# Twelve of sixteen output tiles of a mixer's output projection by the seven-product scheme, with the weight sums added in DRAM

## The chip, the cores and the metric

The kernel runs on one core of one Trainium2 chip. The metric is device time in microseconds (us), the median of several runs. The core has five engines that matter here: TensorE (PE; PEld is its weight load), VectorE (DVE), ScalarE (ACT), GpSimd (POOL) and SyncE (SP, which here only issues DMAs). All arithmetic is in fp32.

## The reference, cut to what matters

One decoder layer on 512 tokens of width 2048: a mixer of three head groups, a cross-attention into 256 memory tokens, and a gated MLP.

```python
def hybrid_mixer(h, w_in, ..., w_out):
    ...
    mixed = jnp.concatenate([o_a, o_b, o_c], axis=-1)     # 512 x 2048
    return mixed @ w_out                                   # w_out 2048 x 2048

mem_n = rms_norm(mem, mem_norm)                            # 256 x 2048
x = x + hybrid_mixer(rms_norm(x, norm_mix), ...)
x = x + memory_cross_attention(rms_norm(x, norm_cross), mem_n, w_cq, w_ckv, w_co)
x = x + conv_ffn(rms_norm(x, norm_ffn), w_up, conv_w, conv_b, w_down)
return rms_norm(x, norm_final)
```

## The kernel before, in words

Activations lie transposed, features on the 128 partitions and tokens along the row, as tiles of 128 x 512. A matmul loads a 128 x 128 block of weights and streams 512 tokens past it. For fp32 accuracy each operand is split in two parts of lower precision (fp32r): a rounded part `hi`, made by ScalarE as a copy, and the rest `lo`, made by VectorE as a subtraction. Each product is then three matmuls (`mm3`, L375 to L377): hi x hi, hi x lo, lo x hi. So each half of a weight tile that comes in (128 x 512, half of a 512 KB DMA) costs one ScalarE and one VectorE operation (`weights` L361 and L362, `split_weights` L336 and L337).

The stages, in order: the input projections; from about 310 us the attention of groups A and B, spread by `tick` between the matmuls of their projections; from 604 us the output projection (`mixer`, its end); the cross-attention (`cross`); the MLP's up projection and its down projection (`ffn`).

**The output projection.** Its 16 output tiles of 128 features each sum over 16 feature tiles of `mixed`. The first half of tiles 0 to 3 runs beside the last attention work; then the attention's memory is closed and the second half of tiles 0 to 3 follows, then tiles 4 to 15 one after the other (`out_units`, two units of 8 blocks each). Each tile is evicted by `evac_o`, which calls `resid` (L1073: VectorE adds the residual x, read from DRAM into a tile `xraw`) and `square` (the sum of squares for the next norm; ScalarE squares, VectorE adds the odd tiles and GpSimd the even ones, L1096). The operands `xo` are the split tiles of `mixed`; they sit in the ring `xp` (`xslot`, tiles `xhi` and `xlo`) that all stages before used for the split x as well.

**The memory's rounding** (`memory`) splits the 16 tiles of the cross-attention's memory (L328, L329), squares them and makes their norm. It is a generator that is advanced one step after each unit from tile 8 on. Its results are needed by the first key tile of the cross-attention (`w_ck`), right after the output projection.

**Queues and buffers.** SP issues the weight loads into a ring of five raw tiles (`WR = 5`, tag `wraw`); the x tiles of the residual use the same ring. Split halves have five buffers each (`WS = 5`). The order on each engine is fixed when the program is built: it follows the order of the program, and an operation that comes later can move up where an engine would be idle and its inputs are there. `issue_after` and `behind` add an order.

**The seven-product scheme.** The MLP's up projection is already computed by it (`up`, `product`): two output tiles, two input tiles and two token halves make a 2 x 2 block product, done with 7 products of 256 tokens in place of 8. It needs sums of weight tiles and sums of token halves. For a few output tiles the weight sums are made ahead in DRAM by DMAs that accumulate, issued by GpSimd, each waiting for the one before (`added`, `up_sums`, L1316); two such sets run at the start of group A's attention (`up_sums(2)` and `up_sums(3)`), one, `up_sums(1)`, behind the sums for the first output tile (`first_sums`, L1362 and L1366), which start with the last square of the output projection. During the cross-attention's output GpSimd also issues accumulating DMAs for squares (L1254).

**Places in memory.** Pools stack from both ends of a partition's memory. A few tiles that nobody reads (`edge`, `ledge`, `rim`, `sill`, `step`) shift what lies behind them by multiples of 32 or 64 bytes.

Of the kernel before, what the change touches and what calls it, by code (L numbers as in the profile page):

```python
# [12 lines left out]
F32 = mybir.dt.float32  # L13
F32R = mybir.dt.float32r
# [5 lines left out]
P = 128  # L20
# [33 lines left out]
EARLY = 4  # L54
BELOW = 3 * PHASE
# [120 lines left out]
def _pack(inp):  # L176
# [26 lines left out]
    a["w_o"] = _units_out(w_out, r(D))  # L203
# [30 lines left out]
class _Trunk:  # L234
    def __init__(self, tc, es, d, out):
# [8 lines left out]
        edge.tile([P, 8], F32, name="edge")  # L244
# [190 lines left out]
    def stats(self, parts, n, name, pool=None):  # L435
# [8 lines left out]
        rs = self.con.tile([P, tl], F32, name="rs" + name)  # L444
        nc.vector.tensor_scalar(rs, ss[:, :tl], 1.0 / D, EPS, op0=ALU.mult, op1=ALU.add)
        nc.gpsimd.tensor_tensor(rs, rs, self.mhalf[:, :tl], op=ALU.pow)

        def spread():
            bc = self.pst("T")
            for t in range(tl):  # L450
                dg = (pool or self.pre).tile([P, P], F32, name="diag", tag="diag", bufs=tl)
                nc.vector.tensor_scalar(dg, self.ident, rs[:, t:t + 1], None, op0=ALU.mult)
                nc.tensor.matmul(bc[:, t * P:(t + 1) * P], self.ones, dg, start=True, stop=True)
            big = (pool or self.con).tile([P, n], F32, name="R", tag="R", bufs=1)
            nc.scalar.activation(big, bc[:, :n], AF.Copy)
            return big

        return rs, spread
# [422 lines left out]
    def mixer(self):  # L881
# [6 lines left out]
        self.vvp = self.pool(es_vv, "vvp", "right")  # L888
        gl = self.pool(es_gl, "gl", "right")
# [90 lines left out]
        for f in range(2, EARLY):  # L980
            self.up_sums(f)
# [17 lines left out]

        def evac_o(dt):  # L1000
            def f(ps):
                self.resid(dt, ps, None, sqs, lambda n: self.mp.tile([P, n], F32, name="sqt", tag="sqt", bufs=2))
            return f
# [9 lines left out]
        units = [self.out_units(d["w_o"], n, xo, evac_o(n), box=box) for n in range(KT)]  # L1013
        self.rate = W_O / 2
        for n in range(0, 4, 2):
# [15 lines left out]
        self.flush()  # L1031
        es_ab.close()
        es_vv.close()
        self.kv = self.pool(self.es_kv, "kv", "right")
        self.kv.tile([P, PHASE], F32, name="ledge")
        self.mp = self.pool(self.es_mp, "mp", "right")
        for n in range(4):
            units[n][1]()
        mem = self.memory()
        for n in range(4, KT):  # L1040
            for u in units[n]:
                u()
                if n >= M0:
                    next(mem, None)
        for _ in mem:
            pass

    def memory(self):

        nc, mp = self.nc, self.mp  # L1050
        parts = [mp.tile([P, MEM], F32, name="msq%d" % i) for i in range(2)]
        self.mem = []
        for k in range(KT):
            if k % 4 == 0:
                four = mp.tile([P, 4, MEM], F32, name="mraw", tag="mraw", bufs=1)
                nc.sync.dma_start(out=four, in_=self.d["memT"][k // 4])
            raw = four[:, k % 4, :]
            hi = mp.tile([P, MEM], F32R, name="mhi%d" % k)
            lo = mp.tile([P, MEM], F32R, name="mlo%d" % k)
            self.mem.append(self.split_to(hi, lo, raw, self.gain(4, k)))  # L1060
            self.square(k, raw, parts, lambda n: mp.tile([P, n], F32, name="msqt", tag="msqt", bufs=2))
            if k % 4 == 3:
                yield
        self.mrs, spread = self.stats(parts, MEM, "m", mp)
        yield
        self.mR = spread()
        yield
# [34 lines left out]
    def cross(self):  # L1102
        nc, d, tc = self.nc, self.d, self.tc
        es = ExitStack()
        kv, mp = self.kv, self.mp
        kh, kl = {}, {}

        def evac_k(h):
            def f(ps):
                kf = mp.tile([P, MEM], F32, name="kf", tag="kf", bufs=2)  # L1110
                nc.vector.tensor_tensor(kf, ps[:, :MEM], self.mR, op=ALU.mult)
                kh[h] = kv.tile([P, MEM], F32R, name="ckh%d" % h)
                kl[h] = kv.tile([P, MEM], F32R, name="ckl%d" % h)
# [4 lines left out]
        vh = [kv.tile([P, S], F32R, name="cvh%d" % i) for i in range(MT)]  # L1118
        vl = [kv.tile([P, S], F32R, name="cvl%d" % i) for i in range(MT)]
# [125 lines left out]
        sx.tile([P, PHASE], F32, name="rim")  # L1245
# [45 lines left out]
        s1, s5 = [self.con.tile([P, HT], F32, name=n) for n in ("s1", "s5")]  # L1291
# [42 lines left out]

    def down_sums(self):
# [18 lines left out]
    def first_sums(self):  # L1354
# [13 lines left out]
        self.up_sums(1)  # L1368
# [496 lines left out]
```

## Time and profile before

| | us |
|---|---|
| median of 3 runs | 2252.03 |
| lowest, highest | 2250.52, 2253.88 |
| profiled execution | 2251.13 |
| its span, first to last instruction | 2249.3 |

| engine | busy, us | share of the span |
|---|---|---|
| TensorE, matmuls | 2232.6 | 99% |
| TensorE, weight loads (beside them) | 2089.9 | 93% |
| VectorE | 1819.5 | 81% |
| ScalarE | 1231.7 | 55% |
| GpSimd | 221.3 | 10% |

The granted clock of TensorE was 0.998 over the span. Busy time of matmuls is a union of overlapping records: the records of a matmul of 256 columns last 277 ns on the mean, though the next one starts after some 114. So the cost of a matmul is read from the distance of starts, or from a count in a window in which TensorE was never idle, not from the mean duration. In rows of groups the two numbers behind the bar are the group's busy time in us and the mean duration in ns; behind the second bar stands the idle time in front of it and what ended it. In rows in order of time the two numbers in front are the start and the duration in us.

### The profile page before, as it was taken

Reading aid. Unit: us, or ns where it says so; the run is one execution under the profiler, and the core shown is the slowest. Engines: PE = TensorE matmul, PEld = TensorE weight load, DVE = VectorE, ACT = ScalarE, POOL = GpSimd, SP = SyncE. Lnnn points to the kernel's source line nnn. Section 1 sums busy time; section 2 is a strip of 40 time slices with the busy share of each in tenths; the row PEclk is TensorE's granted clock in tenths of the full one; section 3 lists DMA queues with packets and bytes.
Section 4 is the critical chain, followed back from the end, with each engine's and each line's share of the span. In section 5 each row is a group of like instructions: output and inputs, shape, how many; then the busy total and the mean of one; then the engine's idle time right before and its main releaser. Section 6 shows DMA issues by size and latency. Waiting matters only on the chain.

```text
span 2249.3 us, 42619 instructions
## 1 busy us (share of the span) xinstructions
PE 2232.6 (99%) x15898; PEld 2089.9 (93%) x15898; DVE 1819.5 (81%) x3587; ACT 1231.7 (55%) x2532; POOL 221.3 (10%) x308
## 2 busy tenths in 40 slices
PE   9999999999999999999999999999999999999997
PEld 8898898888888888889999999999999999999997
DVE  7826756666787356699999999999999999989887
ACT  7324445555575245585555555555555575747563
POOL 2000101000002011121111111111000020101003
PEclk9999999999999999999999999999999999999999
DMA  6422157222224359589777777877534493837542
GB/s 223 162 96 82 49 150 193 97 89 99 78 92 140 122 161 241 134 206 282 198 212 201 221 208 213 215 219 224 173 132 144 145 344 104 305 124 233 186 129 82
DMA packets 141842, 377.09 MB, mean 168 GB/s; under 512 B 14484, under 2 KB 53732, under 8 KB 140932
## 3 DMA queue, kind: packets, MB, share of 16 engines
q1 hardware_dynamic: 90144, 274.18, 35.1%
q0 software_dynamic: 45728, 89.86, 18.2%
q10 hardware_dynamic: 5764, 10.35, 1.3%
q8 instruction: 124, 2.03, 0.4%
q14 instruction: 82, 0.67, 0.1%
HBM read 347.28 MB, written 91.80 MB: 195 GB/s over the span
## 4 chain that ended last, share of the span: by engine, by line
PE 96%; DVE 2%; ACT 1%; DMA 0%; issue 0%; POOL 0%; SPq 0%; DVEq 0%; ACTq 0%
PE acc L375 19%; PE acc L377 19%; PE acc L376 19%; PE psC L375 5%; PE psC L376 5%; PE psC L377 5%; PE acc L416 3%; PE acc L418 3%; PE acc L417 3%; PE psD L377 3%; PE psD L376 3%; PE psD L375 3%; PE psT L556 1%; PE psQ L377 1%; PE psQ L375 1%; PE psQ L376 1%
## 5 line engine op out<-in xcount | busy, mean ns | idle before, releaser
L336 ACT ACTIVATE whi<-wraw 128x512 fp32r<-128x512 f32 (+1 forms) x822 | 471.1, 603 | 407.3 <-PE acc L376 145.0
L337 DVE TENSOR_TENSOR wlo<-wraw,whi 128x512 fp32r<-128x512 f32 (+1 forms) x822 | 522.3, 656 | 65.9 <-ACT whi L336 61.2
L375 PE MATMUL acc<-sum,whi 128*128 128x256 f32 x1956 | 541.8, 277 | 0.4 <-ACT s L1465 0.3
L377 PE MATMUL acc<-sum,wlo 128*128 128x256 f32 x1956 | 541.5, 277 | 0.0
L376 PE MATMUL acc<-sum,whi 128*128 128x256 f32 x1956 | 541.4, 277 | 0.0
L362 DVE TENSOR_TENSOR wlo<-wraw,whi 128x512 fp32r<-128x512 f32 (+2 forms) x328 | 216.1, 665 | 191.2 <-ACT whi L361 188.8
L375 PEld LDWEIGHTS acc<-sum,whi 128*128 128x128 f32 x1956 | 367.2, 188 | 1.0 <-ACT s L1465 0.8
L377 PEld LDWEIGHTS acc<-sum,wlo 128*128 128x128 f32 x1956 | 367.3, 188 | 0.4 <-DVE wlo L337 0.2
L376 PEld LDWEIGHTS acc<-sum,whi 128*128 128x128 f32 x1956 | 367.3, 188 | 0.1
L361 ACT ACTIVATE whi<-wraw 128x512 fp32r<-128x512 f32 (+2 forms) x328 | 198.5, 610 | 284.3 <-PE acc L376 186.5
L375 PE MATMUL acc<-xhi,whi 128*128 128x512 f32 (+1 forms) x848 | 335.1, 395 | 0.5 <-ACT fg L926 0.5
L377 PE MATMUL acc<-xhi,wlo 128*128 128x512 f32 (+1 forms) x848 | 328.4, 387 | 0.0
L376 PE MATMUL acc<-xlo,whi 128*128 128x512 f32 (+1 forms) x848 | 327.9, 387 | 0.0
L375 PE MATMUL psC<-sum,whi 128*128 128x256 f32 x928 | 256.9, 277 | 0.0
L376 PE MATMUL psC<-sum,whi 128*128 128x256 f32 x928 | 256.8, 277 | 0.0
L377 PE MATMUL psC<-sum,wlo 128*128 128x256 f32 x928 | 256.5, 276 | 0.0
L377 PEld LDWEIGHTS acc<-xhi,wlo 128*128 128x128 f32 x848 | 159.3, 188 | 32.5
L375 PEld LDWEIGHTS acc<-xhi,whi 128*128 128x128 f32 x848 | 159.4, 188 | 29.9 <-ACT fg L926 0.9
L376 PEld LDWEIGHTS acc<-xlo,whi 128*128 128x128 f32 x848 | 159.7, 188 | 29.0 <-DVE xlo L324 0.2
L377 PEld LDWEIGHTS psC<-sum,wlo 128*128 128x128 f32 x928 | 174.3, 188 | 0.0
L375 PEld LDWEIGHTS psC<-sum,whi 128*128 128x128 f32 x928 | 174.3, 188 | 0.0
L376 PEld LDWEIGHTS psC<-sum,whi 128*128 128x128 f32 x928 | 174.2, 188 | 0.0
(401 smaller groups left out, 4319.0 us busy)
## 6 DMA issues: line engine op xcount, KB each, us to landing
wraw<-in_w_up SPq DMA_DIRECT2D x125, 512.0 KB, 6.3
b<-in_w_up SPq DMA_DIRECT2D x42, 512.0 KB, 4.5
wraw<-in_w_o SPq DMA_DIRECT2D x32, 512.0 KB, 3.5
wraw<-in_w_d SPq DMA_DIRECT2D x32, 448.0 KB, 4.3
wraw<-in_w_d SPq DMA_DIRECT2D x36, 384.0 KB, 5.0
wraw<-in_w_qka SPq DMA_DIRECT2D x24, 512.0 KB, 3.5
up<-in_w_up POOLq DMA_DIRECT2D x24, 512.0 KB, 7.0
one<-in_w_d POOLq DMA_DIRECT2D x24, 448.0 KB, 6.7
```

Source lines behind the costliest of these rows:

```text
L336: nc.scalar.activation(hi, r, AF.Copy)
L337: nc.vector.tensor_tensor(lo, r, hi.bitcast(F32), op=ALU.subtract)
L361: nc.scalar.activation(hi, r, AF.Copy)
L362: nc.vector.tensor_tensor(lo, r, hi.bitcast(F32), op=ALU.subtract)
L375: nc.tensor.matmul(out, lh, rh, start=start, stop=False, skip_group_check=more)
L376: nc.tensor.matmul(out, lh, rl, start=False, stop=False, skip_group_check=more)
L377: last = nc.tensor.matmul(out, ll, rh, start=False, stop=stop, skip_group_check=more)
L416: self.nc.tensor.matmul(o, xh[:, tt], wh, start=(k == 0), stop=False)
L417: self.nc.tensor.matmul(o, xh[:, tt], wl, start=False, stop=False)
L418: self.last = self.nc.tensor.matmul(o, xl[:, tt], wh, start=False, stop=(k == KT - 1))
L556: nc.tensor.transpose(tp[:, b * P:(b + 1) * P], pt[:, b * P:(b + 1) * P], self.ident)
```

## The change

Tiles 0 to 3 (`PLAIN`) stay as they were. Tiles 4 to 15 become three groups of four (`quad`), each two pairs of output tiles. A pair needs 7 products of 8 blocks x 3 matmuls, with 256 tokens each. The two pairs of a group take turns: product 1 of the first pair, product 1 of the second, and so on.

- The weights' four plain parts come from a new layout `w_p`; the four sums are made in DRAM by `out_sums`, in four sets (two row groups x two column halves) of eight DMAs, at the place where `up_sums(2)` and `up_sums(3)` were. `up_sums(2)` follows them; `up_sums(3)` moves behind `up_sums(1)` in `first_sums`.
- The token sums for products 5, 6 and 3 go to new tiles (`ring`, `low`), and that of product 7 over one half of the `xo` tiles (`place`). `token_turns` makes them in 16 steps: four behind the third plain tile's matmuls, the others while the first group runs, a step after each product. ScalarE copies two or three partial results per pair out of PSUM, VectorE combines the others, and `out` loads x (one tile per output tile, from the raw ring) and adds the residual.
- The groups run their products in the order 1, 2, 4, 5, 6, 3, 7; the last group in the order 5, 6, 3, 7, 1, 2, 4. `memory` now runs in this last group, from its fourth product on in program order, in those tiles; what is left of it runs right behind the group.
- `edge` grows from 8 to 24 floats, and all tiles of `xp` move by 64 bytes; `ledge` in front of `kv` and `rim` go, and a `ledge` of 48 floats is added in the pool `vvp`.

```diff
+PLAIN = 4
+QUADS = (KT - PLAIN) // 4
+LOW = ((5, 3, 0), (5, 3, 1), (3, 3, 0), (3, 3, 1))
+LAST_ORDER = (5, 6, 3, 7, 1, 2, 4)
+OUT_ORDER = (1, 2, 4, 5, 6, 3, 7)
...
-        edge.tile([P, 8], F32, name="edge")
+        edge.tile([P, 8 + PHASE], F32, name="edge")
...
-        for f in range(2, EARLY):
-            self.up_sums(f)
+        self.out_sums()
+        self.up_sums(2)
...
+        for n in range(PLAIN):
+            w = self.weights(d["w_o"][2 * n + 1])
...
+            if n == PLAIN - 2:
+                turns = self.token_turns([self.mix[m] for m in order], xo)
+                for _ in range(4):
+                    next(turns)
+        for n in range(PLAIN):
+            evac_o(n)(box[n])
+        for c in range(QUADS):
+            last = c == QUADS - 1
+            self.quad(PLAIN + 4 * c, LAST_ORDER if last else OUT_ORDER, self.memory() if last else turns)
...
+    def token_turns(self, raw, xo):
...
+        def part(j, v):
+            k = 4 * v
+            if j == 5:
+                a[v] = temp()
+                pair(a[v], lambda i: (raw[k + 2 * i + 1][:, hi], raw[k + 2 * i][:, hi]), ALU.subtract)
...
+            split(j, v)
...
+        def place(v):
+            for i in range(2):
+                th, tl = [t[:, hi] for t in xo[4 * v + 2 * i]]
+                nc.scalar.activation(th, third[v][:, i, :], AF.Copy)
+                tt(tl, third[v][:, i, :], th.bitcast(F32), ALU.subtract)
...
+    def quad(self, d0, order, steps):
...
+        def out(o, i):
+            dt = o["d"] + i
+            t = o["gp" if i else "val"]
+            x1 = self.x1[dt] = self.stream(dt)
+            raw = self.wp.tile([P, S], F32, name="xraw", tag="wraw", bufs=WR, padded_shape=[P, 1024])
+            nc.sync.dma_start(out=raw, in_=self.d["xT"][dt // 2, :, dt % 2, :])
+            tt(x1, raw, t, ALU.subtract if i else ALU.add)
+            self.square(dt, x1, self.sqs, lambda n: t)
...
+        for n, j in enumerate(order):
+            for o in pairs:
...
+                raw = self.up_raw(o["src"][j])
+                parts = self.halves(raw)
+                ps = get(o, where[j], tags[where[j]])
+                for i in range(NP):
+                    th, tl = parts[i // 4]
+                    c = slice(i % 4 * P, (i % 4 + 1) * P)
+                    self.mm3(ps, th[:, c], tl[:, c], *self.operand(j, i), i == 0 and j not in (2, 3, 7),
+                             i == NP - 1 and j not in (), more=True)
...
+                if early or n > 2:
+                    next(steps, None)
...
+    def out_sums(self):
+        w, n = self.d["w_p"], (KT - PLAIN) // 4
...
+            for h in range(2):
+                c = slice(512 * h, 512 * (h + 1))
+                self.added([x[:, c] for x in t], *[x[:, c] for x in b])
...
-        self.up_sums(1)
+        for f in range(1, EARLY, 2):
+            self.up_sums(f)
```

More of the change, by code (lines that the diff above doesn't have):

```diff
@@ L431, in run, with stats @@
         self.rate = 0
-    def stats(self, parts, n, name, pool=None):
+    def stats(self, parts, n, name, new=None):
         nc = self.nc
@@ L1034, in mixer @@
         self.kv = self.pool(self.es_kv, "kv", "right")
-        self.kv.tile([P, PHASE], F32, name="ledge")
         self.mp = self.pool(self.es_mp, "mp", "right")
[L1037 to L1045, printed above, removed]
+        for n in range(PLAIN):
+            w = self.weights(d["w_o"][2 * n + 1])
+            for kk in range(8):
+                wh, wl = w(kk * P, P)
+                self.mm3(box[n], wh, wl, *xo[8 + kk], False, kk == 7)
+            if n == PLAIN - 2:
+                turns = self.token_turns([self.mix[m] for m in order], xo)
+                for _ in range(4):
+                    next(turns)
@@ new lines, in mixer, with tt, temp, pair @@
+        for n in range(PLAIN):
[3 more added lines that the diff above has]
+            self.quad(PLAIN + 4 * c, LAST_ORDER if last else OUT_ORDER, self.memory() if last else turns)
+            if c == 0:
+                for _ in turns:
+                    pass
+    def token_turns(self, raw, xo):
+        nc = self.nc
+        lo, hi = slice(0, HT), slice(HT, S)
+        slots = [(j, v, n) for j in (5, 6, 3) for v in range(NV) for n in range(2)]
+        tok = {s: self.low() for s in LOW}
+        self.mp.tile([P, HALF], F32, name="step")
+        tok.update({s: self.ring() for s in slots if s not in LOW})
+        a, third = {}, {}
+        def tt(out, x, y, op):
+            nc.vector.tensor_tensor(out, x, y, op=op)
+        def temp():
+            return self.spare([P, 2, HT])
+        def pair(out, f, op):
+            for i in range(2):
+                tt(out[:, i, :], *f(i), op)
+        def split(j, v):
+            th, tl = [tok[j, v, n] for n in range(2)]
+            src = a[v].rearrange("p i c -> p (i c)")
+            nc.scalar.activation(th, src, AF.Copy)
+            tt(tl, src, th.bitcast(F32), ALU.subtract)
+        def part(j, v):
[3 more added lines that the diff above has]
+                pair(a[v], lambda i: (raw[k + 2 * i + 1][:, hi], raw[k + 2 * i][:, hi]), ALU.subtract)
+            elif j == 6:
+                pair(a[v], lambda i: (a[v][:, i, :], raw[k + 2 * i][:, lo]), ALU.add)
+            elif j == 3:
+                pair(a[v], lambda i: (a[v][:, i, :], raw[k + 2 * i + 1][:, lo]), ALU.subtract)
+            split(j, v)
+        def seventh(v):
+            third[v] = temp() if v == 0 else a[v]
+            pair(third[v], lambda i: (raw[4 * v + 2 * i][:, hi], raw[4 * v + 2 * i][:, lo]), ALU.subtract)
+        def place(v):
+            for i in range(2):
+                th, tl = [t[:, hi] for t in xo[4 * v + 2 * i]]
+                nc.scalar.activation(th, third[v][:, i, :], AF.Copy)
+                tt(tl, third[v][:, i, :], th.bitcast(F32), ALU.subtract)
+        def operand(j, i):
+            m = slice(i % 2 * HT, (i % 2 + 1) * HT)
+            if j in (5, 6, 3):
+                return [tok[j, i // 2, n][:, m] for n in range(2)]
+            return [t[:, hi if j in (4, 7) else lo] for t in xo[2 * i + (j in (2, 4))]]
+        self.operand = operand
+        for j in (5, 6, 3):
+            part(j, 0)
+            yield
+        seventh(0)
+        yield
+        for j in (5, 6, 3):
+            for v in range(1, NV):
+                part(j, v)
+                yield
+        for v in range(NV):
+            if v:
+                seventh(v)
+            place(v)
+            if v != 2:
+                yield
@@ L1046, in mixer @@
             pass
     def memory(self):
-        nc, mp = self.nc, self.mp
-        parts = [mp.tile([P, MEM], F32, name="msq%d" % i) for i in range(2)]
+        nc = self.nc
+        parts = [self.low(MEM, F32) for _ in range(2)]
         self.mem = []
         for k in range(KT):
[L1054 to L1062, printed above, removed]
+            if k % 2 == 0:
+                two = self.spare([P, 2, MEM])
+                nc.sync.dma_start(out=two, in_=self.d["memT"][k // 4, :, k % 4:k % 4 + 2, :])
+            raw = two[:, k % 2, :]
+            both = self.ring()
+            self.mem.append(self.split_to(both[:, :MEM], both[:, MEM:], raw, self.gain(4, k)))
+            self.square(k, raw, parts, lambda n: self.spare([P, n]))
+            if k % 2:
```

101 lines of the change are left out of this document (85 added, 16 removed).

## The prediction

> **What bounds the kernel now.** I read the page first, for the engines' shares and the chain of work that ended last, then a table by stage over the output projection and over the up projection, which already runs by seven products, and then the order of time on single engines.
>
> ```profile
> span 2249.3 us, 42619 instructions
> PE 2232.6 (99%) x15898; PEld 2089.9 (93%) x15898; DVE 1819.5 (81%) x3587; ACT 1231.7 (55%) x2532; POOL 221.3 (10%) x308
> PE 96%; DVE 2%; ACT 1%; DMA 0%; issue 0%; POOL 0%; SPq 0%; DVEq 0%; ACTq 0%
> ```
> TensorE is busy 99% of the span and makes up 96% of the chain. So a change pays by what it takes from TensorE, as long as nothing makes TensorE wait. The second fence is the table by stage (window, length, then busy time and count for PE, PEld, DVE, ACT, POOL; clock, DMA share, GB/s): eight to nine of the twelve tiles that change, then 200 us of the up projection. Behind it stand two evictions of neighbouring tiles.
>
> ```profile
> 738.00:836.00 98.00, 98.00 (x438) 81.28 (x438) 39.74 (x61) 35.44 (x58) 10.32 (x11) 1.00 0.39 132
> 1100.00:1300.00 200.00, 200.00 (x1760) 200.00 (x1759) 191.23 (x304) 109.26 (x196) 27.29 (x35) 1.00 0.76 212
> ```
> ```profile
> 738.04 0.69 DVE L1073 TENSOR_TENSOR str<-acc,xraw 128x512 f32<-128x512 f32 x1 [1.53 <-PE acc L377]
> 748.92 0.69 DVE L1073 TENSOR_TENSOR str<-acc,xraw 128x512 f32<-128x512 f32 x1 [1.53 <-PE acc L377]
> ```
> In the output projection TensorE is full, VectorE works 40% and ScalarE 36%. A tile takes 748.92 - 738.04 = 10.88 us, 48 matmuls of 512 columns, 227 ns each. In the up projection TensorE is full too, VectorE at 96%, and a matmul of 256 columns takes 200 / 1760 = 113.6 ns, waits included. So half the columns cost half the time here, and TensorE can be kept full by this scheme even beside a VectorE that is all but full.
>
> **What it takes from TensorE.** Removed: 12 tiles x 10.88 = 130.6 us. Added: three groups of four tiles, each two pairs x seven products x 8 blocks x 3 matmuls = 336 matmuls of 256 columns, 1008 in all, x 113.6 = 114.5 us. Saved: 16.1 us. The four plain tiles stay as they are.
> The Trainium skill (TensorE: Matmul & The Clock Gate, "Back-to-back issue gap") gives a lone matmul N/2.4 + 2.5 ns, so two of 256 columns cost more than one of 512; by its figures the saving would be 14.3 us (576 x 215.8 against 1008 x 109.2, an estimate from that page). The rows show no such fixed part: 227 is twice 113.6 within 1 ns.
>
> **What VectorE and ScalarE get.** Per group, 28 weight halves are split in place of 16. Two rows of VectorE's order of time give what one operation costs where they follow each other; the other rows (groups between 690 and 838 us) give what the memory's rounding takes today, and ScalarE's part:
>
> ```profile
> 725.66 1.89 DVE L362 TENSOR_TENSOR wlo<-wraw,whi 128x512 fp32r<-128x512 f32 x3
> 648.52 1.13 DVE L565 TENSOR_TENSOR ptl<-psT,pth 128x256 fp32r<-128x256 f32 x3
> L329 DVE SCALAR_TENSOR_TENSOR mlo<-mraw,gains,mhi 128x256 fp32r<-128x256 f32 x16 | 12.0, 770 | 7.7 <-ACT mhi L328 7.7
> L1096 DVE TENSOR_TENSOR msq<-msq,msqt 128x256 f32<-128x256 f32 x7 | 3.7, 533 | 0.0
> L361 ACT ACTIVATE whi<-wraw 128x512 fp32r<-128x512 f32 x55 | 34.4, 629 | 73.8 <-PE acc L376 73.8
> L328 ACT ACTIVATE mhi<-mraw,gains 128x256 fp32r<-128x256 f32 x16 | 7.8, 498 | 10.7 <-DMA mraw<-in_memT 10.7
> L1094 ACT ACTIVATE msqt<-mraw 128x256 f32<-128x256 f32 x14 | 5.6, 402 | 0.0
> ```
> A VectorE operation of 512 columns takes 1.89 / 3 = 0.63 us, one of 256 1.13 / 3 = 0.38. A group takes TensorE 38.2 us (336 x 113.6). VectorE in it: 28 x 0.63 = 17.6 for splits and 2 x (5 x 0.38 + 3 x 0.63) = 7.6 for combining, residual and odd squares: 25 us. That fits the middle group with room.
> The first group also makes its token sums. Four of sixteen turns are emitted ahead of it; after those come nine parts of two sums and a split (9 x 1.39 = 12.5) and sevenths and places (14 x 0.38 = 5.3): 43 us against 38.2. But the half tiles before it (4 x 24 x 227 ns = 21.8 us of TensorE) hold only about 14 us of VectorE work with their four turns, and the memory's 12.0 + 3.7 us leave that stretch. Together 57 of 60 us: tight, no bound. I take 1 us of waits (0 to 3).
> The last group gets the memory's rounding. It can begin only when product 5 has released its token tiles, 5.5 us into the group; in the 32.7 us left VectorE has 24 x 0.63 + 7.6 + 15.7 = 38 us. So about 5 us spill over the end. The memory's second eight blocks are first needed by the second half of the first key tile, 8 x 3 x 0.1136 = 2.7 us after the group: I take 2 us of wait (0 to 5). ScalarE stays below that: 28 x 0.63 for the splits, 10 x 0.40 or 0.63 for copies and squares (5 us), and 13.4 for the memory, 36 of 38 us.
>
> **The waits at the seams.** A group ends with two x tiles per pair, which sit in the same five raw buffers as the weights (`WR`) and are issued on SP ahead of the next group's weights. What is queued behind them is the next group's first weights, and TensorE waits for those.
>
> ```profile
> wraw<-in_w_up SPq DMA_DIRECT2D x125, 512.0 KB, 6.3
> wraw<-in_w_o SPq DMA_DIRECT2D x32, 512.0 KB, 3.5
> ```
> A product takes 24 x 113.6 = 2.73 us. Count from the start of the last product of the first pair. The five buffers then hold x tiles and the two last weights; the first new weight gets a buffer at about 0, the second when the first x tile is used: 2.73 + 3 x 0.38 + 0.63, with the hops 4.6 us. Landing takes between 3.5 (today here) and 6.3 us (up projection); the groups move 14 x 0.52 + 4 x 0.26 = 8.4 MB in 38 us, 220 GB/s, nearer the up projection's 212 than today's 132, but without its sums in DRAM beside it: I take 4.5. Then 1.3 us of splitting. The second weight is ready at 10.4 and needed at 3 x 2.73 = 8.2. So 2 us at each of the two seams (first to middle, middle to last): 4 us, between 0, if the weights get in first, and 8. The last group gives its x tiles back earlier and has no such seam.
>
> **The sums in DRAM and GpSimd's queue.**
>
> ```profile
> 307.74 0.61 POOL L1316 DMA_DIRECT2D up<-in_w_up  x1
> 388.23 1.02 POOL L1316 DMA_DIRECT2D up<-in_w_up  x1 [6.86 <-DMA up<-in_w_up]
> 691.67 1.42 POOL L1090 TENSOR_TENSOR sq<-str 128x512 f32<-128x512 f32 x1 [302.42 <-DVE str L1073]
> 933.30 1.02 POOL L1316 DMA_DIRECT2D up<-in_w_up  x1 [6.62 <-DMA up<-in_w_up]
> 956.00 0.91 POOL L1254 DMA_DIRECT2D sq<-xsqt  x1 [21.68 <-ACT xsqt L1253]
> ```
> Two sets of eight 512 KB transfers run from 307.7 to about 395: 44 us a set. The new sums are four sets of 768 KB, 44 to 66 us each, and one old set behind them: 308 + 4 x 66 + 44 = 616 at the latest. The first group starts after 712 and GpSimd is idle until 691, so it costs nothing; were the cover gone, the first group would wait for whatever is left of its half. The old set that is moved behind the first sums adds 44 us to GpSimd's queue, from about 926 to 970 in the new time. Queued behind each of its eight waits (up to 7 us) are the accumulations of squares that start at 956 today, and behind those ScalarE, which has three buffers for squares. TensorE holds five split halves of 2.7 us there. I take 0.5 us (0 to 3).
>
> **Where the operands lie.** The edge tile grows by 64 bytes, so every xhi and xlo tile moves by 64 bytes, for the whole mixer. Time from start to start depends on which tile is read:
>
> ```profile
> 760.28 0.39 PE L375 MATMUL acc<-xhi,whi 128*128 128x512 f32 x1
> 760.50 0.39 PE L376 MATMUL acc<-xlo,whi 128*128 128x512 f32 x1
> ...
> 870.03 0.40 PE L416 MATMUL acc<-whi,mhi 128*128 128x512 f32 x1
> 870.26 0.40 PE L417 MATMUL acc<-wlo,mhi 128*128 128x512 f32 x1
> 870.50 0.40 PE L418 MATMUL acc<-whi,mlo 128*128 128x512 f32 x1
> ...
> 936.50 0.28 PE L375 MATMUL acc<-xhi,whi 128*128 128x256 f32 x1
> 936.62 0.28 PE L376 MATMUL acc<-xlo,whi 128*128 128x256 f32 x1
> 936.74 0.28 PE L377 MATMUL acc<-xhi,wlo 128*128 128x256 f32 x1
> ```
> 512 columns take 227 ns with x tiles and 233 (0.47 / 2 and its neighbours) with the memory's; 256 columns take 120 with x tiles at today's place against 113.6 with the sum tiles. Worked out from the pools' sizes, the x tiles come to the same place within 256 bytes as the sum tiles, so I price the groups at 113.6; at 120 for the four products that read x tiles they would cost 576 x 6.4 = 3.7 us more. For the 512-column matmuls that remain no row shows the new place. What matters could be how the tile that is read lies against the weights that are loaded meanwhile, and of such a pair there is one row: behind 598.66 the load fetches attention's qs, which lies 64 bytes further than whi, as far from x as whi will be from the moved x tiles.
>
> ```profile
> 598.66 0.39 PE L377 MATMUL acc<-xhi,wlo 128*128 128x512 f32 x1
> 598.88 0.39 PE L543 MATMUL psS<-kh,qs 128*128 128x512 f32 x1
> ```
> It costs nothing there (0.22). The remaining matmuls, those with x tiles as weights among them, cost between 0 and 6 ns more each, and the last query tile's 96 of 256 columns gain 0.6 us; I take 1 us in all, nearest to this row, and keep the far end as a rival.
>
> **Sum.** -16.1 + 1 + 2 + 4 + 0.5 + 1 = -7.6 us. The profiled execution took 2251.13 us (span 2249.3 and 1.8 around it), 0.9 below the median of the three runs; -7.6 from the median of 2252.0 gives 2244.4 us.
>
> **Rivals.**
> 1. *All waits are covered.* For: TensorE is full in the up projection at a DMA share of 0.76 and VectorE 96%. Against: there no x tiles sit among the weights. Then only the saving counts: 2252.0 - 16.1 = 2236. Chance 0.12.
> 2. *The seams take it.* Landing at 6.3 us makes each seam 4 us, the spill 5, the first group 3, GpSimd's queue 2: 18 against 16, 2252 to 2254, no change. Against: all bounds together. For: they share VectorE. With half of this still within 0.2%. Chance 0.15.
> 3. *The moved x tiles slow the mixer: slower.* 848 x 3 - 576 - 96 = 1872 matmuls of 512 columns keep reading x tiles, and some 960 use them as weights. At the 6 ns that separate the memory's rows from the x rows, and 4.5 for the narrower ones, that is 2064 x 6 + 768 x 4.5 = 15.8 us in place of my 1: 2252.0 - 8.6 + 15.8 = 2259. It decides from 8.6 / 2832 = 3 ns each. For: 233 with tiles 64 bytes off. Against: the row at 598.66. Chance 0.12.
> ```profile
> L375 PE MATMUL acc<-xhi,whi 128*128 128x512 f32 (+1 forms) x848 | 335.1, 395 | 0.5 <-ACT fg L926 0.5
> ```
> 4. *The weight load sets the spacing, not the columns.* Each matmul has its own load; if spacing did not shrink with the columns, 1008 x 227 = 229 us would replace 130.6, and the time be 2350. The up projection's 1760 matmuls with 1759 loads in 200 us exclude it: chance 0.01. The Trainium skill (TensorE: Matmul & The Clock Gate, "Back-to-back issue gap") says that in streams of load and matmul 128 columns take about 81 ns and 512 about 131; a straight line between them would make this change 23 us slower (1008 x 98 against 576 x 131, an estimate from that page). The trace disagrees: 227 for 512, and half of it for 256.
> 5. *The sums come too late*, so that it does not do what it says without a stall: 0.02.
>
> **How the numbers follow.** About 0.2%, 4.5 us, is what a measurement of this kernel can tell from no change. The forecast itself (2239 to 2249) has 0.58; a tenth of that lies within 4.5 us of no change. Faster: 0.52 + 0.12 = 0.64. Same: 0.06 + rival 2 without its upper end, 0.13 = 0.19. Slower: 0.17, from rivals 3, 4, 5 and the rest of 2. The range 2236 to 2256 reaches from rival 1 past rival 2, short of rival 3's full price.
>
> **What would show it.** Right: the twelve tiles take some 114.5 us of matmuls at 113 to 114 ns start to start, with gaps of about 2 us where the middle and the last group start, SP issuing x tiles just ahead of the late weights; VectorE above 90% in the first group; GpSimd's queue empty before 650. Wrong: 512-column matmuls with x tiles at more than 227 ns; a gap of several us at the first key tile; ScalarE held by squares between 930 and 970; no gap at the seams at all.

## The result, and the profile after

The changed kernel takes 2273.59 us (median of five runs, 2271.31 to 2278.62), the kernel before beside it 2252.03. The ratio is 1.0101, 95% interval 1.0086 to 1.0117: 21.6 us slower, where 7.6 us faster was forecast. The profiled execution took 2278.62 us, the longest of the five; its span is 27.4 us above that of before.

From the page of the changed kernel: the span, the busy times, and the chain that ended last.

```profile
span 2276.7 us, 43842 instructions
...
PE 2232.9 (98%) x16330; PEld 2101.9 (92%) x16330; DVE 1877.0 (82%) x3705; ACT 1266.4 (56%) x2608; POOL 266.6 (12%) x340
...
PE 86%; DMA 5%; issue 4%; DVE 3%; ACT 1%; POOL 1%; SPq 0%; DVEq 0%; POOLq 0%; ACTq 0%
```

TensorE was 96% of the chain; now it is 86%, and DMAs, "issue" and VectorE have 12%. So TensorE waits. Where, tells the table by stage of the changed kernel: the three groups (about 715 to 840 us) and what follows (window, length, busy and count for PE, PEld, DVE, ACT and POOL, then granted clock, DMA share, GB/s).

```profile
715.00:754.00 39.00, 39.00 (x338) 38.76 (x337) 32.12 (x63) 23.11 (x47) 2.00 (x1) 1.00 0.54 176
754.00:796.50 42.50, 39.31 (x338) 38.51 (x337) 27.97 (x44) 20.95 (x38) 2.57 (x2) 1.00 0.59 199
796.50:840.00 43.50, 39.94 (x338) 38.76 (x336) 41.82 (x75) 33.73 (x74) 14.71 (x15) 1.00 0.72 247
840.00:860.00 20.00, 3.48 (x28) 3.17 (x27) 5.69 (x14) 6.37 (x12) 4.08 (x4) 0.64 0.82 235
860.00:867.00 7.00, 7.00 (x37) 7.00 (x38) 6.28 (x8) 4.04 (x8) 2.37 (x2) 0.58 0.93 184
```

The first group is full. The second and third have 3 to 4 us of idle TensorE each, and VectorE is nearly full in the third. Then, from 840 to 860 us, TensorE works 3.5 of 20 us, and the 7 us behind that run at a granted clock of 0.58.

To see what each place costs I matched the matmuls of both traces in order of time. There are 16330 - 15898 = 432 more, which is 1008 - 576; so up to the output projection the k-th of one is the k-th of the other, and behind it they match counted from the end, within a few. The plain tiles end at 705.2 us in the kernel before and at 715.0 in the changed one.

| place, start in before, us | later in after by, us | added here |
|---|---|---|
| 583, in the second stream's heads (group B) | 5.0 | 5.0, spread over all stages |
| 604 | 8.6 | 3.6, one stall and the half clock behind it |
| 705, end of the plain tiles | 9.8 | 1.2 |
| 836.4, first key tile, just behind the last group | 4.6 | -5.2, the groups |
| 838.9, a few matmuls later | 21.5 | 16.9, one stall |
| 842.4 | 24.0 | 2.5, low clock |
| 988.5, end of the cross-attention's output | 24.6 | 0.6 |
| 993.4, start of the up projection | 28.3 | 3.7, a stall and low clock |
| last matmul | 27.9 | -0.4 |

**The long stall.** TensorE's order of time in the changed kernel, then GpSimd's:

```profile
842.90 0.28 PE L383 MATMUL acc<-tok,whi 128*128 128x256 f32 x1
843.02 0.28 PE L384 MATMUL acc<-tok,wlo 128*128 128x256 f32 x1
859.81 1.22 PE L460 MATMUL psT<-low,ones 128*128 128x128 f32 x4 [16.52 <-DVE low L459]
```
```profile
834.09 2.09 POOL L1272 TENSOR_TENSOR low<-low,spare 128x256 f32<-128x256 f32 x1 [5.75 <-ACT spare L1270]
836.13 2.00 POOL L1551 DMA_DIRECT2D pre<-in_w_up  x4
842.09 1.09 POOL L1555 DMA_DIRECT2D pre<-in_w_up  x1 [3.95 <-DMA pre<-in_w_up]
856.44 1.03 POOL L1555 DMA_DIRECT2D pre<-in_w_up  x1 [13.27 <-issue]
857.11 1.66 POOL L1272 TENSOR_TENSOR sq<-sq,vg 128x512 f32<-128x512 f32 x1
858.33 1.11 POOL L453 TENSOR_TENSOR rsm<-rsm,mhalf 128x2 f32<-128x2 f32 x1
```

L460 spreads the memory's scale over the partitions. It waits for VectorE's L459, which waits for the 1.1 us operation `rsm` on GpSimd (L453). The method `first_sums` is put behind "the last square that GpSimd added" (`self.pooled`). In the kernel before that was a square of the output projection; now the memory is rounded in the last group, its square at 834 us is the last one recorded, and so the DMAs of the first up projection's sums stand in GpSimd's queue ahead of the last squares of x and of `rsm`. The second accumulating DMA stands at the head of the queue for 13.3 us, since the program makes each wait for the one before, and that one landed 14.0 us after its issue.

**The seams.** What TensorE waited for from 750 to 810 us in the changed kernel (us in total, times, longest):

```profile
PE psC L384 <- DVE wlo L344: 2.4, 3, 1.6
PE acc L384 <- DVE wlo L344: 2.2, 3, 1.5
PE psC L382 <- ACT whi L343: 1.0, 1, 1.0
PE acc L382 <- ACT whi L343: 1.0, 1, 1.0
```

What SP waited for at the first of them, from 735 to 765 us, shows why:

```profile
SPq L1596 <- DVE str L1152: 7.3, 3, 5.5
```

It issues weights (L1596) into buffers that come free only when VectorE has added an x tile (`str`). The split weights are late at two places, the seams between the groups (755 and 798 us), four gaps each. At the first the distances of starts are 1.74, 1.27, 0.54 and 0.75 us; with the usual 0.113 taken off each that is 3.8 us, and 4.0 at the second.

**The 512-column matmuls.** Three neighbours of the plain tiles in the changed kernel start 233 ns apart, where the kernel before had 227:

```profile
700.81 0.39 PE L384 MATMUL acc<-xhi,wlo 128*128 128x512 f32 x1
701.04 0.40 PE L382 MATMUL acc<-xhi,whi 128*128 128x512 f32 x1
701.27 0.39 PE L383 MATMUL acc<-xlo,whi 128*128 128x512 f32 x1
```

### The profile page after: what moved, and what is told of

It is laid out like the page before. It is cut to its first block, busy times and chain, and to the rows that moved or that the text cites. A ratio compares the mean times of both kernels' runs of the same rounds, so it can differ in the third digit from the quotient of the medians.

```text
span 2276.7 us, 43842 instructions
## 1 busy us (share of the span) xinstructions
PE 2232.9 (98%) x16330; PEld 2101.9 (92%) x16330; DVE 1877.0 (82%) x3705; ACT 1266.4 (56%) x2608; POOL 266.6 (12%) x340
## 4 chain that ended last, share of the span: by engine, by line
PE 86%; DMA 5%; issue 4%; DVE 3%; ACT 1%; POOL 1%; SPq 0%; DVEq 0%; POOLq 0%; ACTq 0%
PE acc L382 16%; PE acc L384 16%; PE acc L383 16%; PE psC L384 5%; PE psC L382 5%; PE psC L383 5%; PE psD L382 3%; PE psD L383 3%; PE psD L384 3%; PE acc L423 3%; PE acc L425 3%; PE acc L424 2%; DMA up<-in_w_up 2%; PE psT L563 1%; DMA sq<-xsqt 1%
## 5 line engine op out<-in xcount | busy, mean ns | idle before, releaser
L343 ACT ACTIVATE whi<-wraw 128x512 fp32r<-128x512 f32 (+2 forms) x906 | 522.2, 605 | 438.2 <-PE acc L383 154.4
L344 DVE TENSOR_TENSOR wlo<-wraw,whi 128x512 fp32r<-128x512 f32 (+2 forms) x906 | 582.2, 662 | 81.8 <-ACT whi L343 75.2
L369 DVE TENSOR_TENSOR wlo<-wraw,whi 128x512 fp32r<-128x512 f32 (+2 forms) x280 | 182.2, 658 | 147.8 <-ACT whi L368 145.2
L382 PE MATMUL acc<-xhi,whi 128*128 128x512 f32 (+1 forms) x800 | 302.6, 378 | 1.5 <-ACT whi L343 1.0
L384 PE MATMUL acc<-xhi,wlo 128*128 128x512 f32 (+1 forms) x800 | 296.2, 370 | 2.2 <-DVE wlo L344 2.2
L383 PE MATMUL acc<-xlo,whi 128*128 128x512 f32 (+1 forms) x800 | 296.4, 371 | 0.0
L368 ACT ACTIVATE whi<-wraw 128x512 fp32r<-128x512 f32 (+2 forms) x280 | 168.5, 606 | 225.2 <-PE acc L383 123.2
L384 PEld LDWEIGHTS acc<-xhi,wlo 128*128 128x128 f32 x800 | 150.4, 188 | 30.2 <-DVE wlo L344 2.8
L382 PEld LDWEIGHTS acc<-xhi,whi 128*128 128x128 f32 x800 | 150.5, 188 | 26.5 <-ACT whi L343 1.2
L383 PEld LDWEIGHTS acc<-xlo,whi 128*128 128x128 f32 x800 | 150.7, 188 | 23.8 <-DVE xlo L331 0.3
```

What stands on the lines that cost most here:

```text
L343: nc.scalar.activation(hi, r, AF.Copy)
L344: nc.vector.tensor_tensor(lo, r, hi.bitcast(F32), op=ALU.subtract)
L368: nc.scalar.activation(hi, r, AF.Copy)
L369: nc.vector.tensor_tensor(lo, r, hi.bitcast(F32), op=ALU.subtract)
L382: nc.tensor.matmul(out, lh, rh, start=start, stop=False, skip_group_check=more)
L383: nc.tensor.matmul(out, lh, rl, start=False, stop=False, skip_group_check=more)
```

## The experiments

Four theories, each with a rival: GpSimd's queue makes the long stall and the one at the up projection; the x tiles' new place makes the 5 us that are spread; the raw buffers make the seams; the sums' DMAs make the stall near 600 us. Times are medians, each beside runs of the kernel before on the same chip (2251.6 to 2252.6). Behind each median stand the lowest and highest time, then the ratio to the kernel before and its 95% interval.

### The memory's rsqrt ahead of the sums

```diff
-        nc.gpsimd.tensor_tensor(rs, rs, self.mhalf[:, :tl], op=ALU.pow)
+        self.pooled = nc.gpsimd.tensor_tensor(rs, rs, self.mhalf[:, :tl], op=ALU.pow)
```

> Queue theory: TensorE's 16.8 us stall in front of the memory's scale, and the 2.5 us of lower clock behind it, come from the memory's rsqrt (one small operation on GpSimd) standing behind the DMA waits of the first up projection's sums. Here the sums are issued after that operation, so the stall shrinks to 1 to 4 us. But TensorE then gets to the output of the cross attention some 17 us earlier while the sums and the two sets behind them end some 7 us later, so the squares' DMAs that queue behind them should stall ScalarE and TensorE there by up to 2.5 + 24 us: in all 2262 to 2280, with the stall in another place. Rival (VectorE and ScalarE are late with the memory's rounding, GpSimd's wait is only the last to be seen): the stall stays above 10 us where it is, and the time is 2270 to 2276.

2284.6 us (2282.18 to 2286.03), ratio 1.0142 (1.0127 to 1.0157). The stall at the scale went from 16.8 to 3.7 us (distance of starts), and a new one of 20.7 came at 991 us. GpSimd, ScalarE and TensorE in order of time in this run:

```profile
847.83 1.17 POOL L453 TENSOR_TENSOR rsm<-rsm,mhalf 128x2 f32<-128x2 f32 x1
...
994.35 1.01 POOL L1490 DMA_DIRECT2D up<-in_w_up  x1 [6.56 <-DMA up<-in_w_up]
994.98 2.21 POOL L1428 DMA_DIRECT2D sq<-xsqt  x2
```
```profile
978.87 0.73 ACT L1569 ACTIVATE y<-str,gains 128x512 f32<-128x512 f32 x1
1002.56 0.63 ACT L1427 ACTIVATE xsqt<-str 128x512 f32<-128x512 f32 x1 [22.97 <-DMA sq<-xsqt]
```
```profile
990.87 0.39 PE L384 MATMUL acc<-coh,wlo 128*128 128x512 f32 x1
1011.58 0.77 PE L382 MATMUL acc<-coh,whi 128*128 128x512 f32 x1 [20.32 <-ACT sum L1582]
```

The sums and both sets end at 995 us; only then do the squares' DMAs start. ScalarE has three buffers for squares, stands still for 23 us, and TensorE's weights with it. The mechanism is shown, and the rival (rounding late on VectorE and ScalarE) is out, since the stall at the scale went; the total is 4.6 us above the expected range, because the sets ended 13 us later than in the changed kernel (994 against 981), where I had taken 7, and TensorE ran behind with a low clock once more (0.75 over the next 8 us).

### The fourth up set back in the attention stage

```diff
-        self.up_sums(2)
+        for f in range(2, EARLY):
+            self.up_sums(f)
...
-        for f in range(1, EARLY, 2):
-            self.up_sums(f)
+        self.up_sums(1)
```

> The fourth set of up sums goes back to where it was, into the attention stage behind the second. Queue theory: the stall at the memory's scale stays 17 us; the 2.5 us gap at the first up projection's sums and its 1.5 us of lower clock go, since the squares' DMAs begin some 44 us earlier: 2269, up to 2272 if the set's transfers slow the attention stage. The prediction's view (moving the set costs 0.5 us): 2273, no change.

2275.75 us (2273.15 to 2277.77), ratio 1.0103 (1.0088 to 1.0118): no gain, and 3.8 us above the expected 2272. The long stall stayed (16.8 us) and the gap at the up projection went, as the theory has it (0.1 us are added there in place of 3.7); but with the set's DMAs running until 640 us there is a new gap of 2.75 us at that place. What moving the set cost at the one end it saved at the other.

### Both

> e1 and e2 together. Queue theory: the stall at the memory's scale shrinks to 1 to 4 us and nothing gives it back at the squares, since one set of 44 us less stands ahead of them: 2273.6 - 15 - 2.5 - 4 = 2252, between 2249 and 2256. Rival (rounding late on VectorE and ScalarE): 2268 to 2272.

2265.6 us (2259.22 to 2267.92), ratio 1.0051 (1.0033 to 1.0069). Neither stall is there: 3.7 us are left at the scale, 1.2 at the up projection. It is 8 us less than the changed kernel, where 21 were expected. In the profiled run the stall gave back 13.1 (16.8 to 3.7), its clock 0.6, the up projection 2.0; but the groups took 128.1 us in place of 125.1, since here each seam was followed by a spell of low clock. So the profiled runs differ by 12 us of 21.

```profile
760.00:768.00 8.00, 7.71 (x39) 7.42 (x40) 5.90 (x9) 5.14 (x11) 1.27 (x1) 0.58 0.89 296
```

### The x tiles out of the weights' buffers

```diff
-            raw = self.wp.tile([P, S], F32, name="xraw", tag="wraw", bufs=WR, padded_shape=[P, 1024])
+            raw = self.spare([P, S])
```

`spare` is another ring of buffers, which the weights do not use. First the edit in the changed kernel alone, then with the two edits above:

> The residual's x tiles of the twelve tiles land in the spare ring in place of the weights' five raw buffers. Seam theory: the gaps at the start of the middle and last group, 3.9 us each, go down to at most 0.5 us each, 7 us in all. In this order of GpSimd's queue the memory's rsqrt also stands ahead of the waits, so by the queue theory the 16.8 us stall goes here too, and part or all of it comes back where the squares wait behind the sums: 2250 to 2273. Rival for the seams (weights land too slowly whatever buffers they have): the gaps stay above 2 us each.

> The change with the memory's rsqrt ahead of the sums, the fourth up set back in the attention stage, and the x tiles in the spare ring. Seam theory: against the run without the spare ring (2265.6) the two seams' gaps and the low clock behind them go, 8 to 11 us: 2256, between 2253 and 2259. If the weights were late for another reason: 2264 to 2266.

2274.07 us (2265.44 to 2278.89), ratio 1.0092 (1.0069 to 1.0115), for the first. Between 750 and 800 us TensorE now waited 0.4 us in all, at one place: the seams are gone. The rsqrt stood ahead of the waits in this order, the stall at the scale fell to 2.3 us, and a stall of 16.3 us came at 983, as in the first run. 2259.06 us (2256.1 to 2261.49), ratio 1.0029 (1.0019 to 1.0038), for the second: 6.5 below the run without this edit, where 8 to 11 were expected. The seam theory holds; the buffers, not the landing, made the weights late.

### The x tiles' place by itself

The kernel before with the shift alone:

```diff
-        edge.tile([P, 8], F32, name="edge")
+        edge.tile([P, 8 + PHASE], F32, name="edge")
...
+        self.vvp.tile([P, BELOW], F32, name="ledge")
...
-        self.kv.tile([P, PHASE], F32, name="ledge")
...
-        sx.tile([P, PHASE], F32, name="rim")
```

> The kernel before with one thing of the change: the mixer's x tiles 64 bytes further (edge, ledges and rim as in the change), nothing of the seven products. Address theory: a matmul of 512 columns that reads an x tile takes 233 ns in place of 227, from the first stage on; up to the output projection that makes the 5.8 us that the changed kernel loses there beside its stall at 600 us, and in the sixteen tiles another 768 x 6 ns = 4.6 us: 2252.6 + 10 = 2263, between 2260 and 2265. Rival (the slower matmuls come from the sums' DMAs in the attention stage): 2252 to 2254.

2261.1 us (2260.61 to 2261.48), ratio 1.004 (1.0025 to 1.0055): 8.5 us for 64 bytes. In the output projection, where nothing else differs, starts are 233 ns apart:

```profile
749.36 0.39 PE L376 MATMUL acc<-xlo,whi 128*128 128x512 f32 x1
749.59 0.39 PE L377 MATMUL acc<-xhi,wlo 128*128 128x512 f32 x1
749.82 0.39 PE L375 MATMUL acc<-xhi,whi 128*128 128x512 f32 x1
```

### The x tiles back, in the mended kernel

> As the run before this one, with the x tiles back at their old place. Address theory: 5.8 us come back ahead of the output projection and 0.5 in its four plain tiles, while the four products that read x tiles go from 113.3 to 120 ns, 576 x 6.4 = 3.7 us: 2 to 3 us faster than the run before, 2253 to 2254. Without an effect of the place: the same as the run before.

2251.09 us (2248.72 to 2254.44), ratio 0.9994 (0.9984 to 1.0003): 8 us less, where 2 to 3 were expected. The matmuls that read x tiles do take 120 ns now, as the three rows show; but the groups cost only 1.3 us more in all (122.0 against 120.7), because in the run before half of the first and of the last group's 14 product turns had run at about 118 ns anyway (2.83 us for 24 matmuls). Ahead of the groups the profiled runs differ by 7.6 us.

```profile
719.89 0.28 PE L383 MATMUL acc<-xlo,whi 128*128 128x256 f32 x1
720.01 0.28 PE L384 MATMUL acc<-xhi,wlo 128*128 128x256 f32 x1
720.13 0.28 PE L382 MATMUL acc<-xhi,whi 128*128 128x256 f32 x1
```

### The output projection's sums by themselves

The kernel before with `out_sums` ahead of the up sets, its results unused:

```diff
+        self.out_sums()
         for f in range(2, EARLY):
             self.up_sums(f)
```

> The kernel before with only the output projection's weight sums added in DRAM, unused, ahead of the two up sets in GpSimd's queue. Theory: they slow no matmul, but they are under way where the second stream's heads load their bias rows, so a bias row lands late and TensorE waits 2 to 4 us at 600 us and perhaps once more at 640: 2255 to 2259. Rival 1 (they are free, as the prediction had it): 2252 to 2253. Rival 2 (they also make the 5.8 us of slower matmuls): 2261 to 2264.

2258.48 us (2256.37 to 2263.65), ratio 1.0028 (1.0018 to 1.0039): 5.9 us for DMAs that nobody waits for. The profiled execution took 2263.65 us, the longest of the eight, so its rows hold more of these waits than the median does. VectorE's waits for bias rows between 546 and 690 us, in the kernel before and in this run, and TensorE's order of time in this run:

```profile
DVE ba L596 <- DMA ba<-cdr: 3.8, 4, 1.5
DVE ba L598 <- DMA ba<-cdr: 17.8, 6, 5.8
```
```profile
600.19 0.39 PE L378 MATMUL acc<-xlo,whi 128*128 128x512 f32 x1
602.69 0.60 PE L578 MATMUL psO<-ptl,vv 128*128 128x512 f32 x1 [2.11 <-DVE ptl L567]
```

The second stream's heads (group B of the attention) load a bias row each and use it some 4 to 5 us later; VectorE waits 17.8 us for such rows (3.8 us in the kernel before, over all heads), and TensorE for VectorE. That the late rows are the cause was not yet shown by this.

### Mending what was left

From the version with all four mended (2251.1) two further edits were tried, each alone and both together, and one of them on the kernel before: the memory's rounding one product sooner (`n > 1` for `n > 2`), and each head's bias row asked for ahead of the head's rounding.

> As the run with all four mended (2251.1), with the memory's rounding begun one product sooner in the last group, so that its rsqrt is worked out while the last product still runs. Theory: of the wait that is left at the memory's scale (0.9 and 2.2 us) and its low clock, 2 to 4 us go: 2248, between 2246 and 2250. Rival (VectorE and ScalarE are full in the last group, so that rounding begun sooner only makes the weights later): 2250 to 2253.

> As the run with all four mended, with each head's bias row asked for before the head's rounding in place of after it. Theory: the stalls of 1 to 2.8 us at 595 and 633 us come from bias rows that land late beside the sums' DMAs, so rows asked for sooner take 2 to 4 us away: 2248, between 2246 and 2250. Rival (the sums slow VectorE's or ScalarE's own work there): 2250 to 2252.

> Both of the last two: 2245 if both theories hold, 2248 if one does, 2251 if none.

> The kernel before with bias rows asked for sooner and nothing else, as the measure for the run with both. By the bias theory there is little to gain without the output projection's sums, since VectorE waits 3.8 us in all for these rows and TensorE shows one gap of 0.62 us: 2251 to 2253.

2252.99, 2250.75, 2251.38 and 2251.59 us: no difference in any (ratios 1.0002, 0.9997, 0.9996 and 0.9999 to the kernel before, each interval holding 1). The sooner rounding freed the wait at the scale and made the last group 2.7 us longer (45.7 against 43.0). The bias edit tested nothing: the rows were asked for between 542.7 and 665.2 us, against 542.8 and 663.5 without it. So the DMAs themselves were taken away:

> As the run with all four mended (2251.1), with the second half of the output projection's weight sums left out (their tiles are replaced by the plain weights, so the last six of twelve tiles are computed from wrong operands; the loads and TensorE's work are the same). GpSimd is done with its sums some 120 us sooner, at about 520 us in place of 640, before the second stream's heads begin. Theory: TensorE's stalls at 595 and 633 us come from the sums' DMAs and go, 3 to 5 us: 2247, between 2245 and 2249. Rival (something else of the change makes them): 2250 to 2252.

```diff
-            for h in range(2):
+            for h in range(2 - 2 * g):
...
+            if g:
+                t = [b11, b12, b22, b21]
```

2245.85 us (2244.45 to 2247.03), ratio 0.9976 (0.9966 to 0.9985): the stalls at 595 and 633 us are gone (the largest gap from 550 to 700 us is 0.61 us, 0.62 in the kernel before), VectorE's waits for bias rows are down from 13.6 to 3.8 us, and 5 us of the time went with them. It leaves out half of the sums, so it bounds the gain only.

> As the run with all four mended, with the memory's eight odd square sums moved from VectorE to GpSimd (0.41 us each on VectorE, 0.9 on GpSimd). Theory: in the last group VectorE is the bound (40.99 of 43 us busy), so 8 x 0.41 = 3.3 us less work takes 2 to 3 us off: 2248.5, between 2247 and 2250. Rival (the waits there come from weights or from the memory's tiles that land late): no change, 2250 to 2252.

2254.64 us (2249.88 to 2258.97), ratio 1.0011 (1.0002 to 1.002): not faster, rather a little slower. The last group took 44.7 us against 43.0. VectorE's load is not what sets the last group, or not alone: this theory fell.

### The sums sooner, and a faster kernel

GpSimd has nothing to do from 101 to 205 us, as its order of time in the kernel before shows:

```profile
205.71 1.01 POOL L833 TENSOR_TENSOR kx<-kx,gk 96x384 f32<-96x384 f32 x1 [104.04 <-DVE wlo L362]
```

One set of `out_sums` and one up set go there, behind the first head's last operation; the other sets stay where they were:

```diff
...
+            if h == 0:
+                self.sets = self.out_sums()
+                next(self.sets)
+                self.up_pre = {}
+                self.up_sums(2)
...
```

> As the run with all four mended (2251.1), with nothing left out, but one of the four sets of the output projection's sums and one up set moved into the stretch from 101 to 205 us, where GpSimd has nothing to do. The other four sets should then end at about 540 us, before the second stream's heads begin at 546. Theory: as in the run with half the sums the stalls at 595 and 633 us go: 2246, between 2244 and 2249. Rival (the early sets run past 205 us and hold up the third stream's operations on GpSimd, or the DMAs slow the loads there): 2250 to 2258, with the loss before 310 us.

2246.48 us (2244.04 to 2249.03) against 2251.74, ratio 0.9974 (0.9962 to 0.9985): 5.3 us faster than the kernel before, with the whole computation in place. GpSimd's order of time, VectorE's wait for bias rows from 546 to 690 us, and two stages of the table, all of this run (the last fence begins with the stage from 600 to 690 us of the kernel before and of the changed kernel):

```profile
101.49 1.17 POOL L840 TENSOR_TENSOR kx<-kx,gk 96x384 f32<-96x384 f32 x1 [1.05 <-ACT kx L839]
...
202.51 1.04 POOL L1497 DMA_DIRECT2D up<-in_w_up  x1 [6.57 <-DMA up<-in_w_up]
206.71 1.01 POOL L840 TENSOR_TENSOR kx<-kx,gk 96x384 f32<-96x384 f32 x1 [3.16 <-DVE wlo L369]
...
532.85 1.02 POOL L1497 DMA_DIRECT2D up<-in_w_up  x1 [7.24 <-DMA up<-in_w_up]
```
```profile
DVE ba L603 <- DMA ba<-cdr: 3.2, 4, 1.3
```
```profile
600.00:690.00 90.00, 89.69 (x446) 73.31 (x444) 73.82 (x212) 58.24 (x141) 0.00 (x0) 1.00 0.25 86
600.00:690.00 90.00, 87.70 (x422) 71.62 (x423) 72.39 (x202) 55.10 (x132) 0.00 (x0) 0.98 0.26 84
...
600.00:690.00 90.00, 89.68 (x446) 73.48 (x445) 74.80 (x215) 58.43 (x142) 0.00 (x0) 1.00 0.26 83
690.00:840.00 150.00, 146.00 (x1163) 141.57 (x1162) 130.15 (x230) 98.79 (x196) 29.45 (x24) 1.00 0.67 211
```

GpSimd issues the last DMA of the early sets by 203.5 us, before it is wanted again, and the last of the others by 533.9; the stage from 600 to 690 us is full again (89.7 of 90 us, as in the kernel before; the changed kernel has 87.7). One run more put the last group's x tiles back into the weights' buffers:

> As the run before it, with the last group's x tiles back in the weights' raw buffers, so that only the memory's tiles use the spare ring there. Theory: in the last group ScalarE waited 6.7 us for memory tiles that landed late because the x tiles took their buffers; without them the memory's rounding ends sooner and 1 to 3 us of the group's waits go: 2244. Rival (these waits are covered, or the weights come late in their place): no change against the run before, 2245 to 2247.

2245.26 us (2244.38 to 2249.11), ratio 0.997 (0.9959 to 0.9981): no change that can be told. The group's gaps fell from 2.7 to 1.2 us and the wait at the scale rose from 2.2 to 3.7. ScalarE still waited 6.5 us for the memory's tiles (6.8 in the run before), so it was not the x tiles that made them late.

## Why the prediction was wrong

**What TensorE saves: right.** A product without gaps takes 2.72 us, 113.3 ns a matmul, against 113.6 forecast. The 16.1 us are there; what went wrong are the waits beside it.

**GpSimd's queue: the step that failed.** The prediction asked what moving `up_sums(3)` costs the squares (0.5 us, 0 to 3), and found GpSimd idle when the first group starts. It did not ask what else stands in that queue at the end of the last group. The diff moved the memory's rounding there, and with it the square that `first_sums` is tied to and the rsqrt that the key tile waits for: 16.9 us and 2.5 of low clock behind it, where the sum has 2. "A gap of several us at the first key tile" stood among the signs that would show the forecast wrong; the "2 us of wait" there was worked out from VectorE's load alone. The moved set itself is a size: 3.7 us at the up projection in place of 0.5, and they went when the set was put back. The same step is why mending only the rsqrt made the kernel slower still: the wait sat in the queue, and went to whoever stood behind.

**The sums in DRAM: wrong.** "It costs nothing" rested on the time by which they end, and they did end in time (GpSimd issues its last DMA there at 598 us). What they cost is the time that loads beside them take: from 546 to 604 us the DMA engines are busy 0.76 of the time in place of 0.25, and the bias row asked for at 593 us lands after 6.1 us, its like in the kernel before after 4.2. That is a stall of 2.4 us (start to start) and 3.4 us at half clock behind it, 3.6 us in all here at 600 us, and 5.9 us alone in the kernel before. That their traffic meets small loads that are used 4 to 5 us after they are asked for was not weighed at all. The run without half of them, and the one with them sooner, show it.

**Where the operands lie: a size.** I took 1 us by one row (0.22 us behind attention's `qs`) and kept 15.8 us as a rival with 0.12. It is 6.2 us ahead of the groups here (5.0 and 1.2; 6.2 and 1.2 at the same matmuls in the run with the shift alone), and 8.5 us over that whole run. The rival had the sign and the 6 ns right for the matmuls that stream x tiles past weights; the row at 598.66 was one load, the memory's rows were hundreds. Not all matmuls lose 6 ns: from 604 to 690 us the kernel before has 231 to 234 ns at many places already, and the first stage's narrower ones, with x tiles as weights, stay as they were (384 columns at 173 to 174 ns, 408 at about 186, in both). Why 64 bytes matter is not shown.

**The seams: a size.** 2 us each were taken, 3.8 and 4.0 measured, the upper end. The mechanism was the one foreseen, but the trace has two weights late at each seam, not one: SP's next weights waited for VectorE's use of the x tiles, 7.3 us in three waits from 735 to 765 us.

**The first group and the last.** The first cost 0.7 us over its matmuls, 1 was taken. In the last the scale came 3.7 us late where the queue did not hold it, and 1.8 of low clock behind; 2 were taken (0 to 5).

By the measured terms: -16.1 + 0.7 + 16.9 + 2.5 + 3.7 + 3.6 + 6.2 + 7.8 = 25.3 us; the profiled runs differ by 27.5. Most of the rest lies in the groups, which took 125.1 us: 114.5, 0.7 and 7.8 make 123.0, and the matmuls around the seams' gaps and some products at 114 to 118 ns make the other 2.

With the sums sooner, too, the saving of 16.1 us is worth only 5: 1.3 us go in each of the first two groups, where x tiles are read at 120 ns, some 5 in the last group (43.1 us against 38.2), and 3 at the scale. What sets the last group stays open: neither less work on VectorE, nor sooner rounding, nor other buffers for x took anything off the kernel's time.

## What to carry to other kernels

When a change moves a step, write down every instruction of that step on every queue and look at what is anchored to "the last" of them: an order by position takes along whatever it is tied to. A queue that holds DMA waits gives its delay to whoever stands next; moving one victim ahead only changes the victim, so count what is behind until the queue is empty. DMAs that nobody waits for are not free where small loads with little slack run beside them; find the stretch where their queue and the loads are idle.

## What the runs showed of the hardware

- Half-speed matmuls follow a stall, and not always. Behind the 16.8 us stall the granted clock was 0.5 until 865.9 us (0.58 over the 7 us of the table). In the run with both edits two gaps of 1.7 and 1.3 us, 3 us apart, were followed by 24 matmuls at 213 ns in place of 113, at both seams; in the changed kernel gaps of the same size (1.74 and 1.27 us) left the clock at 1.00. A gap of 2.4 us near 600 us in the changed kernel was followed by 3.4 us at half clock, one of 2.75 us in the run with the set back by none. In the clock records of these runs the stretches at 0.5 inside the kernel last 3.41, 6.83, 17.07 or 20.48 us. The Trainium skill (TensorE: Matmul & The Clock Gate, "Part 1: The HAM clock gate") says that the gate looks at free-running windows of about 3.4 us and so varies from run to run: the traces agree, since these lengths are whole multiples of 3.41. Its advice (the Trainium skill, same page, "Why this matters for your kernels") to avoid gaps above about 3 us is too generous for these traces: 1.7 and 1.3 us were enough in one run.
- The same 64 bytes act in opposite ways: in the output projection matmuls of 512 columns that stream x tiles go from 227 to 233 ns, those of 256 columns from 120 to 113.3.
- Where each accumulating DMA in DRAM (512 or 768 KB) has to wait for the one before, the next one held GpSimd's queue for 4 to 16 us until that one had landed, and with it everything behind it on that engine.
